# Gates taken straight from PSUM by tanh and product, and prompt scores held 2^7 larger, in a two-layer streaming encoder

## The chip, the cores and the metric

The kernel runs on one core of a Trainium2 chip. A core has TensorE (PE: matrix products from SBUF into PSUM), VectorE (DVE), ScalarE (ACT: one function per element, with a scale and a bias), GpSimd (POOL), and SyncE (SP), whose queue issues the DMA transfers here. Each engine works through its own queue in order and waits on semaphores for the others. The metric is the device time of one execution in microseconds.

## The reference

Two attention layers run one after the other on 2048 prompt tokens and 64 sample tokens with 1024 features. Each layer is

```
h = rms_norm(x, norm_g);  q, k, v, gate = split(h @ w_in)
q, k = rms_norm per head (64 wide)
s = q k^T / 8 + bias;  p = softmax(s)           (layer A: with a learned sink per head in the sum)
y = x + ((p v) * silu(gate)) @ w_out
```

Layer A has 16 query heads on 2 key heads; a 64-token chunk sees itself and 2 chunks before it. Layer B has 16 heads each with its own keys, and sees itself and 8 chunks before it. The outputs are y for both kinds of tokens and the newest rows of keys and values. silu(g) is g * (1 + tanh(g / 2)) / 2.

## The kernel before

Every product is made of high and low halves (fp32r pairs in layer A, fp16 pairs in layer B), so a projection of 128 tokens to 512 columns is 24 matmuls (`project`, lines 679 to 681). Layer A goes through four head groups `qd`, each over all units of 256 tokens; the first of them (`qd` 0) projects keys and values too, so that there a 256-column k/v projection and a 512-column q/gate projection alternate. Layer B goes through eight head pairs `hp`, each over all units; one projection gives q, k, v and gate of two heads, 128 columns each. Both write into the PSUM tile `pj`, of which there are two banks.

**The order of the work.** TensorE's order is written out by hand: attention steps of item x, and between them projection matmuls of later items (`filler.to`). All other engines' orders are set by a scheduler that simulates the program. Small side tasks (splitting weights, normalising heads, the gate) go through a list, `bg.put(cost, fn)`, with a cost each; `bg.share` runs some of it at each attention step, urgent ones first, and `queries` or `scores` force what an item still lacks.

**From the projection to the scores.** In layer A, `evacuate` (L702) copies q and gate from `pj` to `pa` and `pb`, scaled by the token's RMS factor `rr` on ScalarE. In layer B, `evacuate_b` copies q and k to `pa` (L715), the value's high half (L719), the value's low half on VectorE (L720), and then the gate to `pb` (L723). The scheduler's tool orders any two engines that touch one PSUM bank, so these four follow one another where the engine changes. `head_norm` squares on POOL (L756), sums on VectorE (L757), raises to -1/2 on POOL (L761) and multiplies on VectorE (L774). `gate` is a tanh of `pb` into a buffer `sq` on ScalarE (L782) and a product (tanh + 1) * gate on VectorE (L783).

`queries` transposes normalised q and k on TensorE (L844, tile `tp`) and writes them as fp16 halves with factors `qf`, `kf` per feature. `scores` in each layer makes the products (L1139 and L1140; L1416 and L1417, tile `sb`), adds the bias and takes the minimum of the negated scores in one VectorE instruction with a constant scale of 1.0 (L1150, L1420, results `p` and `nm`), and exponentiates on ScalarE (L1156, L1429). The row sums `sm` are inverted (L1161, L1437; in layer B, L1440 multiplies some by 2^14), and POOL multiplies them into the gate (`G`: L1163, L1448). The probabilities are transposed by TensorE (into `sa` or `sb`, split by L813, L814, L816, L817) or, for one head of each pair, split by L1463 and POOL's L1464 and transposed by DMA. `sb` has two buffers, for scores, transposed probabilities and transposed gates together.

`constants` (lines 136 to 154) makes the factors at the start; `scale_work` runs `input_across`, `input_scales` and `everywhere` once for each head pair, beside the work of the pair before. `bias_vectors_a` and `bias_vectors_b` make the negated bias vectors once.

Of the kernel before, what the change touches and what calls it, by code (L numbers as in the profile page):

```python
# [12 lines left out]
I32 = mybir.dt.int32  # L13
AF = mybir.ActivationFunctionType
# [42 lines left out]
def hybrid_encoder_kernel(  # L57
# [70 lines left out]
    qf = const([P, 2], "qf")  # L128
    kf = const([P, 2], "kf")
    kgr = const([P, 2, 2 * HD], "kgr")  # L130
    sink = const([P, 16], "sink")
    nsink = const([P, 16], "nsink")
    tab = const([P, 16], "tab")
    held = {}

    def constants():
# [8 lines left out]
        nc.vector.tensor_tensor(qf, qsc, ksc, op=ALU.mult)  # L145
        nc.vector.tensor_scalar(kf.bitcast(I32), qf.bitcast(I32), 0x7F800000, None, op0=ALU.bitwise_and)
        nc.vector.tensor_scalar(kf, kf, 0.125, 1.0, op0=ALU.mult, op1=ALU.max)
        nc.vector.tensor_scalar(kf, kf, 2.0 ** 15, 1.0, op0=ALU.min, op1=ALU.mult)
        inv = t("ms", [P, 8])[:, 0:2]
        nc.vector.reciprocal(inv, kf)  # L150
        nc.vector.tensor_tensor(qf, qf, inv, op=ALU.mult)
        nc.vector.tensor_scalar(qf, qf, 60000.0, -60000.0, op0=ALU.min, op1=ALU.max)
# [5 lines left out]
    scl = const([P, 9, 3], "scl")  # L158
    gsb = const([P, 8, KC], "gsb")
    S_W, C_B, G_B = (lambda h, i=i: scl[:, h, i : i + 1] for i in range(3))  # L160
    S_WO, S_OG, C_O = (scl[:, 8, i : i + 1] for i in range(3))
# [22 lines left out]

    def times(dst, a, c):
        nc.vector.tensor_scalar(dst, a, c, 1.0, op0=ALU.mult, op1=ALU.mult)

    def largest(j, a, b):
# [20 lines left out]

    def everywhere(h, o):  # L210
        ps = psum("tp", 512, 1)
        nc.tensor.matmul(ps[:, 0:3], ones[0:1, 0:1].to_broadcast([1, P]), o, start=True, stop=True)
        nc.vector.tensor_copy(scl[:, h], ps[:, 0:3])

# [5 lines left out]
    def input_across(h):  # L220
        across(h, h + 1)
        e, r, o = row[:, 16:17], row[:, 17:18], row[:, 20:23]
        powers(row[:, h : h + 1], e, r)
        times(o[:, 0:1], r, WB_)
        times(o[:, 1:2], e, 1 / (HB * WB_))
        times(o[:, 2:3], e, 0.5 / VB if h > 0 and len(TURNED) == 2 else 0.5 / (VB * PB))

    def input_scales(h):
        everywhere(h, row[:, 20:23])
        nc.vector.tensor_scalar(gsb[:, h], gain[:, 1, :], S_W(h), 1.0, op0=ALU.mult, op1=ALU.mult)  # L230
# [57 lines left out]
    def bias_vectors_a():  # L288
        oh = held["oh"]
        ps = psum("tp", 512, 1)  # L290
        nc.tensor.matmul(ps[:16, :VL], tab[:32, :16], oh[:32, :VL], start=True, stop=True)
        held["va"] = va = t("row", [P, VL], 2)
        nc.vector.tensor_scalar(va[:16, :VL], ps[:16, :VL], -1.0, 1.0, op0=ALU.mult, op1=ALU.mult)

    def bias_vectors_b():
        held["vb"] = vb = t("res", [P, 2 * OT], 2)
        vr = t("res", [P, 2 * OT], 2)
        load(vr[:16, :257], rel_rev)
        nc.vector.memset(vb[:16, 0:127], 0.0)
        nc.vector.tensor_scalar(  # L300
            vb[:16, 127:383], vr[:16, 0:256], vr[:16, 0:1], -1.0, op0=ALU.subtract, op1=ALU.mult
        )

    def keep(layer):
# [116 lines left out]

    bg = Background()

    def load_weights(g, *specs, scale=None):
# [183 lines left out]

    rr = [const([P, NT + 1], f"rms{l}") for l in range(2)]

    def token_scales(unit, x, ps):
# [7 lines left out]
    def sums_to_scales(layer, tt, parts, ps):  # L619
        w = len(parts)  # L620
        for i, part in enumerate(parts):
            nc.tensor.matmul(ps[:, 2 * i : 2 * i + 2], part, ones, start=True, stop=True)
        v = t("ms", [P, 8])
        nc.vector.tensor_scalar(
            v[:, : 2 * w], ps[:, : 2 * w], 1.0 / D, EPS, op0=ALU.mult, op1=ALU.add
        )
        nc.gpsimd.tensor_tensor(
            rr[layer][:, tt : tt + w],
            v[:, : 2 * w].rearrange("p (i e) -> p i e", e=2)[:, :, 0],
            mhalf[:, :w],  # L630
            op=ALU.pow,
        )

    def token_rows(unit):
# [11 lines left out]
    def row_scales(unit):  # L646
# [17 lines left out]
        nc.vector.tensor_scalar(v[:, :w], v[:, :w], 1.0 / D, EPS, op0=ALU.mult, op1=ALU.add)  # L664
        nc.gpsimd.tensor_tensor(rr[0][:, tt : tt + w], v[:, :w], mhalf[:, :w], op=ALU.pow)

    def project(tile_, xc, w, C, res, ps=None):
# [19 lines left out]

    def evacuate(layer, tt, n, ps, C, G, b=None):
        a = t("pa", [P, 384], 4)
        pieces = [(a[:, : C - G], ps[:, : C - G])]  # L690
        if G:
            out = a
            if b is None:
                b = t("pb", [P, 256], 5)
                out = a, b
            pieces.append((b[:, :G], ps[:, C - G : C]))
        else:
            out = a
        sc = rr[layer][:, tt : tt + 1]
        for dst, src in pieces:  # L700
            if n == P:
                held["evac"] = nc.scalar.activation(dst, src, AF.Identity, scale=sc).ins  # L702
            else:
                nc.scalar.activation(dst[:n], src[n:], AF.Identity, scale=sc[n:])
        if n < P:
            for dst, src in pieces:
                nc.vector.scalar_tensor_tensor(
                    dst[:n], src[:n], sc[:n], dst[:n], op0=ALU.mult, op1=ALU.add
                )
        return out  # L710

    def evacuate_b(hp, tt, ps, g):
        a = t("pa", [P, 384], 4)
        true = a if tt >= NT - 4 else a[:, 0:256]
        nc.scalar.activation(true, ps[:, : true.shape[1]], AF.Identity, scale=C_B(hp))  # L715
# [3 lines left out]
        nc.scalar.activation(vh[:, :, 0:HD], v, AF.Identity, scale=c)  # L719
        nc.vector.scalar_tensor_tensor(  # L720
            vh[:, :, HD:P], v, c, vh[:, :, 0:HD], op0=ALU.mult, op1=ALU.subtract
        )
        held["evac"] = nc.scalar.activation(g, ps[:, 384:512], AF.Identity, scale=C_B(hp)).ins  # L723
        return a
# [120 lines left out]

    halves = [slice(0, 64), slice(64, 128)]

    QS = const([P, 4, P], "QS", F32R)
# [62 lines left out]
    def layer_a():  # L911
# [4 lines left out]
        def add_unit(qd, place, unit):  # L916
# [193 lines left out]
        def scores(it):  # L1110
# [33 lines left out]
            for j in range(2):  # L1144
# [4 lines left out]
                for h in (2 * j, 2 * j + 1):  # L1149
                    mi = nc.vector.tensor_tensor_reduce(  # L1150
                        out=pv[:n, h % 2, :nk], in0=Sv[h][:n, :nk], in1=bias[h][:n, b0 : b0 + nk],
                        op0=ALU.add, op1=ALU.min, scale=1.0,
                        scalar=nsink[:n, 4 * qd + h : 4 * qd + h + 1], accum_out=nm[:n, h : h + 1],
# [6 lines left out]
            bg.anchor(mi, ex)  # L1160
            nc.vector.reciprocal(sm[:n], sm[:n])  # L1161
            it.G = G = t("G", [P, 256])
            nc.gpsimd.tensor_tensor(  # L1163
# [92 lines left out]
    def layer_b():  # L1256
# [4 lines left out]
        def add_unit(hp, unit):  # L1261
# [21 lines left out]
            def gen():  # L1283
# [9 lines left out]
                for e, (tt, t0, n) in enumerate(tiles):  # L1293
# [89 lines left out]
        def scores(it, i, h):  # L1383
# [35 lines left out]
            for r, b, c in soft:  # L1419
                mi = nc.vector.tensor_tensor_reduce(  # L1420
                    out=p[r, :nk], in0=S[r, o : o + nk], in1=b,
                    op0=ALU.add, op1=ALU.min, scale=1.0, scalar=3e38, accum_out=it.nm[r, c : c + 1],
                )
# [12 lines left out]
            if c == w - 1:  # L1436
                nc.vector.reciprocal(it.sm[:n, :w], it.sm[:n, :w])  # L1437
                if turned(it, 0) and len(TURNED) == 1:
                    part = it.sm[:n, TURNED[0] : w : 2]
                    nc.vector.tensor_scalar(part, part, PB, 1.0, op0=ALU.mult, op1=ALU.mult)  # L1440
                it.G = G = t("G", [P, 256])
# [480 lines left out]
```

## Time and profile before

| | us |
|---|---|
| median of 3 runs | 2210.4 (2204.73 to 2212.95) |
| the profiled execution | 2214.94 |
| its span | 2213.1 |
| TensorE busy | 2102.7 |
| VectorE busy | 1563.9 |
| ScalarE busy | 1425.7 |
| POOL busy | 1004.9 |

Layer A's attention runs from about 50 to 700 us, its output projection to about 850, layer B's attention from 870 to 2030, and the last output projection to the end. In rows of groups the columns are: line, engine, operation, output and inputs by name, shapes and count, then total busy us and mean ns of one, then the engine's idle time just before them and what ended it. In rows of waits: the engine and line that waited, for which engine and line, us in total, how often, and the longest.

### The profile page before, as it was taken

How to read it: one execution, taken by the hardware profiler on the slowest of the kernel's cores; microseconds unless marked ns; L12 is line 12 of the kernel's file. 1: busy time of each engine (PE TensorE's matmuls, PEld its weight loads, DVE VectorE, ACT ScalarE, POOL GpSimd, SP SyncE). 2: the span in 40 equal slices, each digit the busy share in tenths (PEclk: the TensorE clock that was granted, in tenths of full speed). 3: DMA queues.
4: the chain of work that ended last, by engine and by line, in shares of the span. 5: the costliest groups of instructions: out<-in, count | busy, mean ns of one | idle time of the engine just before them, and what ended most of it. 6: DMA issues, size and time to landing. Idle time of an engine off the chain costs nothing. (4 is left out here: it accounts for less than half of the span.)

```text
span 2213.1 us, 41369 instructions
## 1 busy us (share of the span) xinstructions
PE 2102.7 (95%) x13441; PEld 1522.1 (69%) x13441; DVE 1563.9 (71%) x4105; ACT 1425.7 (64%) x3610; POOL 1004.9 (45%) x1509
## 2 busy tenths in 40 slices
PE   7999999999999999989999999999999998998999
PEld 6887888788889997556555555555555555556888
DVE  6769777677676456778676777877767778677642
ACT  6878878777785333666666766766667667576420
POOL 5645544334454455853444444444454445443000
PEclk9999999999999999999999999999999999999999
DMA  8856546856546667545465565654756546345664
GB/s 274 275 162 215 179 127 219 234 160 195 170 129 184 210 204 244 171 143 167 107 186 133 130 177 130 173 148 121 186 133 155 159 111 172 91 104 136 199 200 124
DMA packets 383096, 372.87 MB, mean 168 GB/s; under 512 B 174672, under 2 KB 320352, under 8 KB 382848
## 3 DMA queue, kind: packets, MB, share of 16 engines
q1 hardware_dynamic: 382880, 370.23, 58.0%
q8 instruction: 106, 1.74, 0.3%
q14 instruction: 110, 0.90, 0.1%
HBM read 257.59 MB, written 73.43 MB: 150 GB/s over the span
## 5 line engine op out<-in xcount | busy, mean ns | idle before, releaser
L679 PE MATMUL pj<-wh,xx 128*128 128x512 f16 (+2 forms) x1648 | 643.4, 390 | 5.8 <-ACT pb L702 4.1
L681 PE MATMUL pj<-wh,xx 128*128 128x512 f16 (+2 forms) x1648 | 625.5, 380 | 2.5 <-POOL xx L564 2.5
L680 PE MATMUL pj<-wh,xx 128*128 128x512 f16 x1024 | 391.5, 382 | 0.0
L1429 ACT ACTIVATE p<-p,nm 128x640 f32<-128x640 f32 (+5 forms) x264 | 198.9, 753 | 213.6 <-DVE nm L1420 108.0
L1765 PE MATMUL pj<-xx,wh 128*128 128x264 f32 (+1 forms) x1024 | 290.0, 283 | 8.5 <-DVE res L1775 4.1
L1766 PE MATMUL pj<-xx,wh 128*128 128x264 f32 (+1 forms) x1024 | 287.7, 281 | 0.0
L1464 POOL TENSOR_TENSOR values<-p,values 128x640 f16<-128x640 f32 (+2 forms) x112 | 140.0, 1250 | 243.5 <-ACT values L1463 243.5
L680 PE MATMUL pj<-wl,xx 128*128 128x512 f32 (+1 forms) x624 | 233.9, 375 | 2.2 <-DVE wl L470 2.2
L564 POOL TENSOR_TENSOR xx<-xraw,xx 128x528 fp32r<-128x528 f32 (+4 forms) x144 | 184.9, 1303 | 87.8 <-ACT xx L563 74.6
L1420 DVE CUSTOM_DVE_ANT_0 p<-sb,BT 128x640 f32<-128x640 f32 (+5 forms) x272 | 195.6, 719 | 38.3 <-PE sb L1417 35.6
L1250 POOL TENSOR_TENSOR o<-gt,o 128x256 f32<-128x256 f32 (+1 forms) x132 | 101.1, 766 | 206.2 <-ACT p L1156 89.6
L761 POOL TENSOR_TENSOR f<-f,mhalf 128x4 f32<-128x4 f32 (+2 forms) x187 | 187.0, 1000 | 13.8
L681 PEld LDWEIGHTS <-xx 128*128 128x128 f16 x1024 | 100.9, 99 | 125.9 <-issue 3.9
L774 DVE TENSOR_TENSOR pa<-pa,f 128x256 f32<-128x256 f32 (+3 forms) x221 | 136.5, 618 | 55.1 <-POOL f L761 50.6
L1156 ACT ACTIVATE p<-p,nm 128x257 f32<-128x257 f32 (+2 forms) x272 | 134.3, 497 | 50.1 <-DVE nm L1150 41.7
L756 POOL TENSOR_TENSOR sq<-pa 128x256 f32<-128x256 f32 (+2 forms) x187 | 123.7, 663 | 72.5 <-ACT pa L715 38.2
L679 PEld LDWEIGHTS <-xx 128*128 128x128 f16 x1024 | 101.0, 99 | 71.5 <-issue 2.7
L680 PEld LDWEIGHTS <-xx 128*128 128x128 f16 x1024 | 100.9, 99 | 70.3 <-issue 2.9
L817 DVE SCALAR_TENSOR_TENSOR pl<-sb,ph 128x640 f16<-128x640 f32 (+4 forms) x144 | 106.2, 737 | 58.2 <-ACT ph L816 56.5
L1767 PE MATMUL pj<-xx,wl 128*128 128x264 f32 x512 | 145.0, 283 | 1.0 <-DVE wl L463 1.0
L1767 PE MATMUL pj<-xx,wh 128*128 128x264 f16 x512 | 142.1, 277 | 1.3 <-DVE wh L460 1.3
L1150 DVE CUSTOM_DVE_ANT_0 p<-sa,BT,nsink 128x256 f32<-128x256 f32 (+2 forms) x272 | 117.3, 467 | 34.6 <-PE sa L844 29.5
(273 smaller groups left out, 5290.7 us busy)
## 6 DMA issues: line engine op xcount, KB each, us to landing
xx<-xsb SPq DMA_DIRECT2D x112, 512.0 KB, 4.2
xx<-xsa SPq DMA_DIRECT2D x88, 512.0 KB, 4.8
xraw<-oga SPq DMA_DIRECT2D x64, 264.0 KB, 3.6
xraw<-ogb SPq DMA_DIRECT2D x64, 264.0 KB, 3.6
xsa<-xx SPq DMA_DIRECT2D x32, 512.0 KB, 4.0
scan<-in_w_in_b_dram SPq DMA_DIRECT2D x64, 256.0 KB, 4.6
wl<-in_w_in_b_dram SPq DMA_DIRECT2D x64, 256.0 KB, 4.0
xraw<-in_x_dram SPq DMA_DIRECT2D x40, 256.0 KB, 3.9
```

The lines of the kernel that those rows point to most:

```text
L564: nc.gpsimd.tensor_tensor(lo, rv, wide(hi), op=ALU.subtract)
L679: nc.tensor.matmul(ps[:n, :C], xh, wh, start=k == 0, stop=False)
L680: nc.tensor.matmul(ps[:n, :C], xh, wl, start=False, stop=False)
L681: nc.tensor.matmul(ps[:n, :C], xl, wh, start=False, stop=k == KC - 1)
L761: nc.gpsimd.tensor_tensor(fv, fv, mhalf[:n, :H], op=ALU.pow)
L774: nc.vector.tensor_tensor(sv, sv, fv.unsqueeze(2).to_broadcast([n, H, HD]), op=ALU.mult)
L1420: mi = nc.vector.tensor_tensor_reduce(out=p[r, :nk], in0=S[r, o : o + nk], in1=b, op0=ALU.add, op1=ALU.min, scale=1.0, scalar=3e38, accum_ ...
L1429: ex = nc.scalar.activation(p[:n, :nk], p[:n, :nk], AF.Exp, scale=-1.0, bias=it.nm[:n, c : c + 1], accum_out=it.sm[:n, c : c + 1],)
L1464: lo = nc.gpsimd.tensor_tensor(two[:, :, 1, :], pv, two[:, :, 0, :], op=ALU.subtract)
L1765: nc.tensor.matmul(ps[:, :OT], wh, oh, start=k == 0, stop=False)
L1766: nc.tensor.matmul(ps[:, :OT], wh, ol, start=False, stop=False)
L1767: nc.tensor.matmul(ps[:, :OT], wl, oh, start=False, stop=k == KC - 1)
```

## The change

1. **Gates.** For whole 128-token tiles the copy of the gate is gone. `gate_of` takes tanh on ScalarE straight from `pj` into a new buffer `e` (one of it), and VectorE multiplies (tanh plus or minus 1) with the gate, again straight from `pj`. The missing scale is put elsewhere: in layer A the tanh's scale is `nhalf`, which POOL makes from `rr` (`halve`), and the row sums get a factor -`rr`; in layer B the tanh's scale is a fourth column `H_B` of the scales, and the factor G_B, which already multiplies the transposed gate, takes the rest. In layer A the order stays q then gate; in layer B gate comes first, then q and k, then v. Side tasks `gate` remain only for tiles with fewer tokens. The 2^14 on the row sums (L1440) moves into G_B.
2. **Scores.** Factors `up`, `down` and `nup` are worked out at the start from the largest gains (a power of two, at most 2^7). q and the bias vectors are multiplied by `up`; the score reduction's scale becomes `down`, one value per partition, in place of 1.0. The factor's limits for `kf` change with it.

```
+        both = t("res", [P, 2 * OT], 2)[:, : 4 * P].rearrange("p (d c) -> p d c", c=4)
+        load(both, qk_gain.partition_broadcast(P))
+        nc.vector.tensor_tensor(both[:, :, 0:2], both[:, :, 0:2], both[:, :, 2:4], op=ALU.mult)
+        nc.vector.tensor_reduce(
+            up, both[:, :, 0:2].rearrange("p d c -> p c d"), axis=AX.X, op=ALU.max,
+            apply_absolute_value=True,
+        )
+        exponent(up, up)
+        nc.vector.tensor_scalar(up, up, 2.0 ** 10, 1e-20, op0=ALU.mult, op1=ALU.max)
+        nc.vector.reciprocal(up, up)
+        nc.vector.tensor_scalar(up, up, 2.0 ** 29 * 2.0 ** 7, 2.0 ** 7, op0=ALU.mult, op1=ALU.min)
+        nc.vector.reciprocal(down, up)
+        times(nup, up, -1.0)
+        nc.vector.tensor_tensor(qsc, qsc, up, op=ALU.mult)
...
     def everywhere(h, o):
...
+        if 0 < h < 8 and len(TURNED) == 1:
+            r = scl[halves[TURNED[0]], h, 2:3]
+            times(r, r, PB)
...
+    def halve(tt, w):
+        nc.gpsimd.tensor_tensor(nhalf[:, tt : tt + w], rr[0][:, tt : tt + w], mhalf[:, :w], op=ALU.mult)
...
+    def gate_of(ps, scale, g, one=1.0):
+        W = g.shape[1]
+        e = t("e", [P, 256], 1)[:, :W]
+        held["evac"] = nc.scalar.activation(e, ps, AF.Tanh, scale=scale).ins
+        nc.vector.scalar_tensor_tensor(g, e, one, ps, op0=ALU.add, op1=ALU.mult)
+
+    def evacuate(layer, tt, n, ps, C, G):
         a = t("pa", [P, 384], 4)
+        b = t("pb", [P, 256], 5) if G else None
+        sc = rr[layer][:, tt : tt + 1]
+        if n == P:
+            held["evac"] = nc.scalar.activation(a[:, : C - G], ps[:, : C - G], AF.Identity, scale=sc).ins
+            if G:
+                gate_of(ps[:, C - G : C], nhalf[:, tt : tt + 1], b[:, :G], -1.0)
+            return (a, b) if G else a
...
     def evacuate_b(hp, tt, ps, g):
         a = t("pa", [P, 384], 4)
         true = a if tt >= NT - 4 else a[:, 0:256]
+        gate_of(ps[:, 384:512], H_B(hp), g)
         nc.scalar.activation(true, ps[:, : true.shape[1]], AF.Identity, scale=C_B(hp))
...
-        held["evac"] = nc.scalar.activation(g, ps[:, 384:512], AF.Identity, scale=C_B(hp)).ins
...
-                it.todo += head_norm(n, it.pr[:n, 0:256], qd > 0) + gate(n, it.gate[:n])
+                it.todo += head_norm(n, it.pr[:n, 0:256], qd > 0)
+                if n < P:
+                    it.todo += gate(n, it.gate[:n])
...
-                        op0=ALU.add, op1=ALU.min, scale=1.0,
+                        op0=ALU.add, op1=ALU.min, scale=down[:n, 0:1],
...
+            if n == P:
+                nc.vector.tensor_scalar(
+                    sm, sm, rr[0][:, tt : tt + 1], -1.0, op0=ALU.mult, op1=ALU.mult
+                )
...
-                    it.todo += head_norm(n, pr[:n, 0:256]) + gate(n, it.gate[:n, e])
+                    it.todo += head_norm(n, pr[:n, 0:256])
...
-                    op0=ALU.add, op1=ALU.min, scale=1.0, scalar=3e38, accum_out=it.nm[r, c : c + 1],
+                    op0=ALU.add, op1=ALU.min, scale=down[r, 1:2], scalar=3e38, accum_out=it.nm[r, c : c + 1],
...
-                if turned(it, 0) and len(TURNED) == 1:
-                    part = it.sm[:n, TURNED[0] : w : 2]
-                    nc.vector.tensor_scalar(part, part, PB, 1.0, op0=ALU.mult, op1=ALU.mult)
```

More of the change, by code (lines that the diff above doesn't have):

```diff
@@ L134, in hybrid_encoder_kernel, with times, exponent @@
     held = {}
+    def times(dst, a, c):
+        nc.vector.tensor_scalar(dst, a, c, 1.0, op0=ALU.mult, op1=ALU.mult)
+    def exponent(dst, a):
+        nc.vector.tensor_scalar(
+            dst.bitcast(I32), a.bitcast(I32), 0x7F800000, None, op0=ALU.bitwise_and
+        )
     def constants():
@@ L157, in hybrid_encoder_kernel @@
     top = const([P, 12], "top")
-    scl = const([P, 9, 3], "scl")
+    scl = const([P, 9, 4], "scl")
     gsb = const([P, 8, KC], "gsb")
-    S_W, C_B, G_B = (lambda h, i=i: scl[:, h, i : i + 1] for i in range(3))
+    S_W, C_B, G_B, H_B = (lambda h, i=i: scl[:, h, i : i + 1] for i in range(4))
     S_WO, S_OG, C_O = (scl[:, 8, i : i + 1] for i in range(3))
@@ L210, in everywhere @@
     def everywhere(h, o):
+        w = o.shape[1]
         ps = psum("tp", 512, 1)
-        nc.tensor.matmul(ps[:, 0:3], ones[0:1, 0:1].to_broadcast([1, P]), o, start=True, stop=True)
-        nc.vector.tensor_copy(scl[:, h], ps[:, 0:3])
+        nc.tensor.matmul(ps[:, :w], ones[0:1, 0:1].to_broadcast([1, P]), o, start=True, stop=True)
+        nc.vector.tensor_copy(scl[:, h, :w], ps[:, :w])
+        if 0 < h < 8 and len(TURNED) == 1:
+            r = scl[halves[TURNED[0]], h, 2:3]
+            times(r, r, PB)
     def input_top(h):
@@ L221, in input_across @@
         across(h, h + 1)
-        e, r, o = row[:, 16:17], row[:, 17:18], row[:, 20:23]
+        e, r, o = row[:, 16:17], row[:, 17:18], row[:, 20:24]
         powers(row[:, h : h + 1], e, r)
@@ L225, in input_across @@
         times(o[:, 1:2], e, 1 / (HB * WB_))
-        times(o[:, 2:3], e, 0.5 / VB if h > 0 and len(TURNED) == 2 else 0.5 / (VB * PB))
+        times(o[:, 2:3], o[:, 1:2], 0.5 / VB if h > 0 and len(TURNED) == 2 else 0.5 / (VB * PB))
+        nc.vector.tensor_tensor(o[:, 2:3], o[:, 2:3], e, op=ALU.mult)
+        times(o[:, 3:4], o[:, 1:2], 0.5)
     def input_scales(h):
-        everywhere(h, row[:, 20:23])
+        everywhere(h, row[:, 20:24])
         nc.vector.tensor_scalar(gsb[:, h], gain[:, 1, :], S_W(h), 1.0, op0=ALU.mult, op1=ALU.mult)
@@ L422, in hybrid_encoder_kernel @@
     bg = Background()
+    halves = [slice(0, 64), slice(64, 128)]
     def load_weights(g, *specs, scale=None):
@@ L632, in sums_to_scales @@
         )
+        if layer == 0:
+            halve(tt, w)
     def token_rows(unit):
@@ L665, in row_scales @@
         nc.gpsimd.tensor_tensor(rr[0][:, tt : tt + w], v[:, :w], mhalf[:, :w], op=ALU.pow)
+        halve(tt, w)
     def project(tile_, xc, w, C, res, ps=None):
@@ L686, in project @@
         return cost
-    def evacuate(layer, tt, n, ps, C, G, b=None):
-        a = t("pa", [P, 384], 4)
+    def gate_of(ps, scale, g, one=1.0):
[4 more added lines that the diff above has]
+    def evacuate(layer, tt, n, ps, C, G):
+        a = t("pa", [P, 384], 4)
+        b = t("pb", [P, 256], 5) if G else None
[5 more added lines that the diff above has]
+            return (a, b) if G else a
         pieces = [(a[:, : C - G], ps[:, : C - G])]
         if G:
[L692 to L695, printed above, removed]
             pieces.append((b[:, :G], ps[:, C - G : C]))
-        else:
-            out = a
-        sc = rr[layer][:, tt : tt + 1]
         for dst, src in pieces:
[L701 to L710, printed above, removed]
+            nc.scalar.activation(dst[:n], src[n:], AF.Identity, scale=sc[n:])
+        for dst, src in pieces:
+            nc.vector.scalar_tensor_tensor(
+                dst[:n], src[:n], sc[:n], dst[:n], op0=ALU.mult, op1=ALU.add
+            )
+        return (a, b) if G else a
     def evacuate_b(hp, tt, ps, g):
```

24 lines of the change are left out of this document (14 added, 10 removed).

## The prediction

> **What bounds the kernel now.** I read the page's engine totals first, then busy time by stage, then whom TensorE waited for, then the groups by shape that the change touches, and last the timelines of the start and of one normalisation chain.
>
> The page, engine totals and granted clock:
>
> ```profile
> span 2213.1 us, 41369 instructions
> PE 2102.7 (95%) x13441; PEld 1522.1 (69%) x13441; DVE 1563.9 (71%) x4105; ACT 1425.7 (64%) x3610; POOL 1004.9 (45%) x1509
> PEclk9999999999999999999999999999999999999999
> ```
>
> TensorE is busy 2102.7 of 2213.1 us at full clock; the change adds or removes no matmul of a projection, score or output. So it can only move the 110.4 us in which TensorE stands. Where these lie (columns: stretch, its length, busy time of PE, PEld, DVE, ACT, POOL with instruction counts, clock, DMA share, GB/s):
>
> ```profile
> 0.00:50.00 50.00, 36.30 (x197) 29.97 (x198) 36.45 (x114) 33.82 (x77) 28.39 (x43) 0.97 0.88 279
> 50.00:200.00 150.00, 145.85 (x896) 123.47 (x895) 107.45 (x404) 121.22 (x339) 83.71 (x127) 0.99 0.68 215
> 200.00:700.00 500.00, 494.73 (x2848) 407.67 (x2847) 371.01 (x1070) 385.98 (x1065) 231.73 (x425) 1.00 0.59 179
> 870.00:2030.00 1160.00, 1090.34 (x6680) 654.19 (x6681) 872.26 (x2212) 772.18 (x1942) 569.04 (x837) 0.99 0.55 147
> ```
>
> Start-up: 13.7 us idle. Layer A from 200 on: 5.3, nothing to win. Layer B's attention: 69.7 us. Who let TensorE go, in layer B (870 to 2030) and then before 200 us:
>
> ```profile
> PE sb L844 <- DVE nm L1420: 14.0, 7, 2.3
> PE sb L1416 <- DVE nm L1420: 12.7, 10, 1.7
> PE sb L844 <- DVE pl L817: 10.2, 14, 1.4
> PE tp L844 <- DVE pa L774: 9.4, 7, 1.7
> ...
> PE sb L844 <- ACT values L719: 2.3, 1, 2.3
> ...
> PE tp L844 <- ACT gt L1237: 1.7, 2, 1.5
> PE sb L844 <- ACT gt L1237: 1.5, 3, 0.9
> ```
>
> ```profile
> PE pj L679 <- ACT pb L702: 4.1, 3, 2.1
> ...
> PE pj L680 <- DVE wl L470: 2.2, 1, 2.2
> ```
>
> In layer B it is VectorE that ends the waits: scores reduced (L1420), low halves (L817), normalised q/k (L774). ScalarE ends 5.5 us of them. So time taken off ScalarE pays only through VectorE's queue, and time put on VectorE can cost directly.
>
> **ScalarE, part by part.** Rows of the groups (busy us, mean ns | idle before):
>
> ```profile
> L723 ACT ACTIVATE pb<-pj,scl 128x128 f32<-128x128 f32 x128 | 46.6, 364 | 63.7 <-DVE values L720 60.9 <-DVE scrow L202 1.2
> L782 ACT ACTIVATE sq<-pb 128x128 f32<-128x128 f32 x128 | 38.4, 300 | 0.6
> L702 ACT ACTIVATE pb<-pj,rms 128x256 f32<-128x256 f32 x64 | 30.1, 470 | 0.0
> L782 ACT ACTIVATE sq<-pb 128x256 f32<-128x256 f32 x64 | 26.8, 419 | 2.8 <-DVE f L765 1.6
> ```
>
> Each 128-token tile had a gate evacuation and, later, a tanh of the copy. Now one tanh reads PSUM with a scale read per partition. I price it as the evacuation it replaces (same shape, same kind of scale): 364 ns in B, 470 in A. So the old tanhs' price leaves: 128 x 300 ns + 64 x 419 ns = 65.2 us less ScalarE, 38.4 of it in B.
>
> **VectorE.** Rows of its groups:
>
> ```profile
> L783 DVE SCALAR_TENSOR_TENSOR pb<-sq,pb 128x128 f32<-128x128 f32 x128 | 55.6, 434 | 20.5 <-ACT sq L782 20.3
> L720 DVE SCALAR_TENSOR_TENSOR values<-pj,values 128x128 f16<-128x128 f32 x128 | 36.5, 285 | 2.9 <-ACT values L719 1.4
> L783 DVE SCALAR_TENSOR_TENSOR pb<-sq,pb 128x256 f32<-128x256 f32 x64 | 32.6, 510 | 12.8 <-ACT sq L782 12.2
> L1771 DVE SCALAR_TENSOR_TENSOR res<-pj,scl,res 128x264 f32<-128x264 f32 x64 | 31.1, 490 | 71.7 <-PE pj L1767 50.4 <-DMA res<-x 20.8
> L1775 DVE TENSOR_TENSOR res<-pj,res 128x264 f32<-128x264 f32 x64 | 27.0, 427 | 52.9 <-PE pj L1767 52.8
> L1150 DVE CUSTOM_DVE_ANT_0 p<-sa,BT,nsink 128x256 f32<-128x256 f32 x240 | 106.4, 479 | 31.2 <-PE sa L844 27.3 <-PE sa L1140 1.9
> L1420 DVE CUSTOM_DVE_ANT_0 p<-sb,BT 128x256 f32<-128x256 f32 x16 | 6.7, 419 | 0.2
> L1440 DVE TENSOR_SCALAR sm<-sm 128x2 f32<-128x2 f32 x56 | 10.0, 178 | 1.3
> ```
>
> The product (tanh+1) times gate had two SBUF inputs; now one input is PSUM. The nearest rows with a PSUM input: 285 ns for 128 columns (L720) against 434, 427 for 264 columns (L1775) against 510. That is 128 x 149 + 64 x 83 ns = 24.4 us less. [...] The rows here are means amid other work and I take them.
>
> The scale of the score reduction turns from the constant 1.0 into a value per partition. L1150, which has one such operand, costs 60 ns more than L1420 at the same 256 columns; L1771 against L1775 says 63. At 63 ns for 272 calls that is 17.1 us in each layer (in A it is the second such operand: 0 to 63, I take 63). The new factor on sm in A: 64 x 178 ns = 11.4; the one removed in B: 10.0. Sums: A 17.1 + 11.4 - 5.3 = +23.2; B 17.1 - 10.0 - 19.1 = -12.0 us. A's 23 hide beside TensorE, which stood only 5.3 us after 200. In B only what stands on a wait counts: 17 waits name L1420, 17 x 0.063 = **+1.1** (0 to 17.1, every call on the path).
>
> **ScalarE's relief in B**, 38.4 us of 772. Direct waits on it are 5.5 us, and the L817 waits (10.2) follow a ScalarE cast; I take a fifth of these 15.7: **-3** (0 to -18, half of the 36.9 of the three uppermost waits).
>
> **Order and release in B.** The order was q/k evacuation, v, v's low half on VectorE, gate. Now it is tanh, product on VectorE, q/k, v, low half. L723's row shows that ScalarE does not read the bank while VectorE does: it stood 60.9 us behind L720, 0.48 per tile over 128. So q/k now come later by a tanh, a product and such a wait: 0.36 + 0.29 + 0.48 = 1.13 us. Queued behind the waiting evacuation are v's and the exponentials; behind the q/k are POOL's squares, the factor and L774, for which TensorE waited 7 times. One such chain, ScalarE, POOL, VectorE and TensorE rows:
>
> ```profile
> 1177.59 0.47 ACT L715 ACTIVATE pa<-pj,scl 128x256 f32<-128x256 f32 x1
> ...
> 1181.09 1.40 POOL L1464 TENSOR_TENSOR values<-p,values 128x640 f16<-128x640 f32 x1 [7.04 <-ACT values L1463]
> 1182.44 1.19 POOL L756 TENSOR_TENSOR sq<-pa 128x256 f32<-128x256 f32 x2
> ...
> 1186.91 0.69 DVE L175 TENSOR_REDUCE most<-scan 128x1 f32<-128x512 f32 x1 [1.92 <-DMA scan<-in_w_in_b_dram]
> 1187.52 0.60 DVE L774 TENSOR_TENSOR pa<-pa,f 128x256 f32<-128x256 f32 x1
> ...
> 1188.17 0.44 PE L844 MATMUL tp<-ident,pa 128*128 128x128 f32 x2 [1.58 <-DVE pa L774]
> ```
>
> Here the square stood over 4 us behind POOL's L1464 and L774 behind a scan's transfer: q/k 1.13 later would cost nothing. So half of 7 x 1.13: **+4** (0, to 15 items paying it whole, 17).
>
> [...]
>
> **Release in A.** The projection's bank was free after ScalarE's gate copy (L702 pb); now after VectorE's product. In the first quarter k/v and q/gate projections alternate on two banks, and TensorE already waited 3 times for pb. Each grows by product and queue, 0.43 + 0.48 = 0.9: **+3** (-1.4, a third of the 4.1, as ScalarE reaches it earlier; to 15, all 17 tiles). Layer A's q copy still comes first there, so its chain does not move.
>
> **Start-up.** Nine more VectorE instructions in `constants`, two of 256 elements, and one 256 KB load. Where VectorE is on the path:
>
> ```profile
> 12.44 0.15 DVE L145 TENSOR_TENSOR qf<-qsc,ksc 128x2 f32<-128x2 f32 x1
> ...
> 14.12 0.40 DVE L591 TENSOR_TENSOR o<-res 128x256 f32<-128x256 f32 x1
> ...
> 24.70 1.52 DVE L591 TENSOR_TENSOR o<-res 128x256 f32<-128x256 f32 x1
> ```
>
> 7 x 0.16 + 2 x 0.40 = 1.9, in a stage where TensorE stood 2.2 us for VectorE's wl (L470). **+2** (0 if they fall into a gap; 4.1 with the 1.52 rows, plus 0.9 for 256 KB at 279 GB/s: 5). The extra load is one more issue on SP's queue ahead of weights, inside that 0.9. POOL's `halve`, nine small products, lies before the tanh alone, after q's evacuation: 0. The few 1x1 operations per head pair and the extra products on the bias vectors: 0, a unit ahead of their use.
>
> **Sum:** 2 + 3 + 4 + 1.1 - 3 = +7.1 us. The profiled execution took 2214.94 us (span 2213.1 and 1.8 around it), 4.5 above the median 2210.4 of the runs shown; against it the sum gives 2222.0, against the median 2217.5: I say **2217**.
>
> **Rivals.** One, slower: the hand-over ScalarE, VectorE, ScalarE stands on TensorE's path in B. Price 1.13 us per item; I count 3.5 items, from 7 the sum passes 0.5%, and 15 give 17 for my 4, a sum of +20: about 2231. For it: 7 waits already there, 60.9 us of the same hand-over; against it: the chain above.
>
> Two, faster: ScalarE's relief reaches VectorE's queue, whose casts come sooner, and halves the 36.9 us of B's three largest waits: -18.5 in place of -3, and release and order cost nothing (+3 left): 2195. For it stands how long VectorE waited for ScalarE's casts in B:
>
> ```profile
> DVE pl L817 <- ACT ph L816: 55.0, 58, 1.8
> ```
>
> Against it: ScalarE was idle a third of B, so its work rarely came late through load.
>
> Three, no effect: both engines idle enough to take up every shift, only start-up's 2 remains: 2212.
>
> **Chances.** Forecast 0.36 (0.06 of it past the upper 0.5%), slower rival 0.34, faster rival 0.20 (0.02 within), no effect 0.10. About 0.5%, 11 us, is what a measurement of this kernel can tell from no change. Slower 0.06 + 0.34 = 0.40; faster 0.18; within 0.30 + 0.10 + 0.02 = 0.42. The forecast's own range is 2207 to 2226; the wide one, 2196 to 2239, leaves out a tenth at each end.
>
> **What would show it.** ScalarE's busy time falls by about 65 us; no evacuation into pb and no tanh from pb is left for whole tiles. The reductions into nm cost 60 ns more; if not, the 1.1 goes. The q/k evacuation (pa from pj) in B waits on the product instead of L723 on values; the product's mean lies near 285 in B. If TensorE's waits for normalised pa in B stay under 14 us, the hand-over is covered; above 25 it is rival one. Waits for nm and pl falling below 25 us speak for rival two. The forecast fails if the order that the scheduler gives VectorE's and ScalarE's queues shifts by more than these terms.

## The result and the profile after

The changed kernel takes 2234.1 us (median of 6 runs, 2224.1 to 2240.4) where the kernel before takes 2209.1 (median of 6, 2204.7 to 2213.3): a ratio of 1.0109, 95% interval [1.0082, 1.0136], about 24 us slower. The profiled execution took 2234.35 us. In the experiments below every ratio is to the kernel before, run beside it on the same chip, since the median of the kernel before itself lies between 2209 and 2221 from one set of runs to the next.

The page's engine totals of the changed kernel:

```profile
span 2232.6 us, 41200 instructions
PE 2113.7 (95%) x13441; PEld 1527.0 (68%) x13441; DVE 1576.1 (71%) x4146; ACT 1383.0 (62%) x3418; POOL 994.1 (45%) x1518
```

ScalarE has 192 instructions fewer, VectorE is 12 us busier (the prediction's A +23.2 and B -12.0 make 11.2), the matmuls are the same 13441. Yet TensorE is busy 11.0 us longer; the rest of the span's +19.5, 8.5 us, is idle time.

As TensorE's order is written out by hand, the n-th matmul is the same one in both traces, and the difference of their starts, each counted from the start of its span, tells when time is lost: +3.5 us at 50 us, +1.8 at 200, +4.5 at 870, +16.8 at 960, +22.2 at 2030, +19.4 at the last matmul. So 12.3 us go in 90 us, at the start of layer B's first head pair. Busy time in this stretch, in the columns of the prediction, first of the changed kernel, then of the kernel before:

```profile
870.00:960.00 90.00, 71.71 (x375) 39.37 (x374) 58.39 (x124) 42.37 (x106) 55.66 (x64) 0.89 0.54 182
```

```profile
870.00:960.00 90.00, 80.36 (x449) 45.62 (x450) 66.11 (x148) 52.56 (x136) 66.45 (x77) 0.94 0.55 182
```

Every engine does less in it, 74 matmuls fewer on TensorE, and the clock is lower, 0.89 against 0.94. Whom TensorE waited for, in the changed kernel, over the whole span (us in total, times, longest):

```profile
PE tp L884 <- DVE pa L814: 20.0, 7, 9.0
PE sb L1460 <- DVE nm L1464: 16.0, 13, 2.0
...
PE tp L884 <- DVE scl L236: 8.3, 5, 2.0
```

The same two waits for `pa` and `scl` in the kernel before:

```profile
PE tp L844 <- DVE pa L774: 11.0, 8, 1.7
...
PE tp L844 <- DVE scl L213: 1.3, 5, 0.3
```

The wait for normalised q/k (L774 before, L814 now) rose from 11.0 to 20.0 us, and one of its 7 waits is 9.0. The wait for `scl` (the copy of the next head pair's scales out of PSUM, where they have been spread over the partitions; L213 before, L236 now) was 1.3 us in 5 and is 8.3. Here is the 9.0. The rows of its chain on POOL, VectorE and TensorE, from the changed kernel's timeline:

```profile
903.12 0.41 DVE L797 TENSOR_REDUCE f<-sq 128x4 f32<-128x256 f32 x1
904.89 1.27 POOL L591 TENSOR_TENSOR xraw<-xraw,rows 128x512 f32<-128x512 f32 x1 [2.85 <-DMA xraw<-x]
906.11 1.16 POOL L595 TENSOR_TENSOR xx<-xraw,xx 128x512 f16<-128x512 f32 x1
907.22 0.21 POOL L800 TENSOR_TENSOR f<-f,small 128x4 f32<-128x4 f32 x1
907.37 3.38 POOL L595 TENSOR_TENSOR xx<-xraw,xx 128x512 f16<-128x512 f32 x3
910.70 1.02 POOL L801 TENSOR_TENSOR f<-f,mhalf 128x4 f32<-128x4 f32 x1
911.75 0.83 DVE L814 TENSOR_TENSOR pa<-pa,f 128x256 f32<-128x256 f32 x1 [3.60 <-POOL f L801]
912.73 0.66 PE L884 MATMUL tp<-ident,pa 128*128 128x128 f32 x2 [8.99 <-DVE pa L814]
```

And POOL and TensorE at the same tile in the kernel before:

```profile
895.08 0.24 POOL L760 TENSOR_TENSOR f<-f,small 128x4 f32<-128x4 f32 x1
895.40 1.01 POOL L761 TENSOR_TENSOR f<-f,mhalf 128x4 f32<-128x4 f32 x1
897.12 1.27 POOL L560 TENSOR_TENSOR xraw<-xraw,rows 128x512 f32<-128x512 f32 x1 [0.72 <-DMA xraw<-x]
```

```profile
898.80 0.44 PE L844 MATMUL tp<-ident,pa 128*128 128x128 f32 x2 [0.87 <-DVE pa L774]
```

Before, the two tiny POOL steps of the head norm (an addition and the power -1/2, on 4 columns) came first, and the scaling and splitting of the next tokens (L560, L564) followed. Now the scheduler has put them the other way round: the sum is ready at 903.5, but the addition waits till 907.2 behind a product that itself stands 2.85 us for its transfer, and the power behind three splits, till 910.7. Some 7 us of a chain that holds 1.2 us of POOL's work, and TensorE stands at its end.

The second place occurs in later head pairs, where the next pair's scales are spread; four times the copy stands as shown here. VectorE and TensorE, changed kernel:

```profile
1407.85 1.61 DVE L814 TENSOR_TENSOR pa<-pa,f 128x256 f32<-128x256 f32 x1 [1.40 <-POOL f L801]
1409.38 0.15 DVE L236 COPY scl<-tp 128x4 f32<-128x4 f32 x1
```

```profile
1409.59 0.66 PE L884 MATMUL tp<-ident,pa 128*128 128x128 f32 x4 [2.01 <-DVE scl L236]
```

The copy of 0.15 us frees the one PSUM tile `tp` for the next transposes. It stands behind a normalisation that waits for POOL and then runs 1.61 us; TensorE waits for the copy. In the kernel before, the instruction ahead of the copy at these places is a sum of 0.42 us (L757).

### The profile page after: what moved, and what is told of

Its sections match the earlier page's. It is cut to its first block, busy times and chain, and to the rows that moved or that the text cites. A ratio compares the mean times of both kernels' runs of the same rounds, so it can differ in the third digit from the quotient of the medians.

```text
span 2232.6 us, 41200 instructions
## 1 busy us (share of the span) xinstructions
PE 2113.7 (95%) x13441; PEld 1527.0 (68%) x13441; DVE 1576.1 (71%) x4146; ACT 1383.0 (62%) x3418; POOL 994.1 (45%) x1518
## 4 chain that ended last, share of the span: by engine, by line
PE 44%; DVE 12%; DMA 7%; ACT 6%; issue 4%; POOL 4%; SPq 1%; POOLq 0%; ACTq 0%; DVEq 0%
PE pj L717 6%; PE pj L719 6%; PE pj L718 6%; DMA scan<-in_w_in_b_dram 4%; PE pj L1806 4%; PE pj L1808 4%; PE pj L1807 4%; DVE p L1464 2%; PE sb L884 2%; PE o L1641 2%; PE sb L1460 1%; DVE pa L814 1%; PE sb L1461 1%; PE o L1602 1%; ACT p L1473 1%
## 5 line engine op out<-in xcount | busy, mean ns | idle before, releaser
L1464 DVE CUSTOM_DVE_ANT_0 p<-sb,BT,down 128x640 f32<-128x640 f32 (+5 forms) x272 | 211.9, 779 | 28.0 <-PE sb L1461 25.1
L796 POOL TENSOR_TENSOR sq<-pa 128x256 f32<-128x256 f32 (+2 forms) x187 | 117.5, 630 | 169.7 <-ACT pa L756 101.9
L814 DVE TENSOR_TENSOR pa<-pa,f 128x256 f32<-128x256 f32 (+3 forms) x221 | 124.7, 564 | 49.8 <-POOL f L801 45.5
L1190 DVE CUSTOM_DVE_ANT_0 p<-sa,BT,nsink 128x256 f32<-128x256 f32 (+2 forms) x272 | 134.3, 528 | 21.3 <-PE sa L884 17.6
```

The costliest lines, as they stand in the source:

```text
L814: nc.vector.tensor_tensor(sv, sv, fv.unsqueeze(2).to_broadcast([n, H, HD]), op=ALU.mult)
L1464: mi = nc.vector.tensor_tensor_reduce(out=p[r, :nk], in0=S[r, o : o + nk], in1=b, op0=ALU.add, op1=ALU.min, scale=down[r, 1:2], scalar=3e3 ...
```

## The experiments

The first theory is that gate-first in layer B costs by moving tiny instructions in the in-order queues, not by its own durations. The rivals are the scores' new work, layer A's later release of the projection bank, and the hand-over itself (the prediction's 1.13 us per item). The expectations of the first four runs use the word "hand-over" for the later q/k together with the long wait that grows from it, and set a "reshuffle" against it: any shift of the queues makes a stall somewhere.

**Gate last in B.** All of the change, with layer B's gate in its old place:

```
     def evacuate_b(hp, tt, ps, g):
...
-        gate_of(ps[:, 384:512], H_B(hp), g)
         nc.scalar.activation(true, ps[:, : true.shape[1]], AF.Identity, scale=C_B(hp))
...
+        gate_of(ps[:, 384:512], H_B(hp), g)
         return a
```

> The changed kernel with one line moved: in layer B tanh and product come last, after q/k, v and v's low half, where the gate copy stood before. Theory hand-over (q/k come later by a tanh, a product and a wait, and one such delay near 900 us grows to the 9.0 us wait and a half clock): some 12 us less than the change, about 2222 us, no TensorE wait over 4 us for normalised pa. Theory score scale (the per-partition scale and the longer start cost the time): as the changed kernel, 2234. Theory reshuffle (any shift of the queues makes such a stall somewhere): anything, with a long wait at another place.

Measured: 2211.0 us, ratio 0.9969 [0.9958, 0.9980]. The same instructions in another order are 1.4% faster than the changed kernel (0.9969 against 1.0109) and beat the kernel before. That is 28 to 31 us for the place of the gate, where some 12 were expected, so more than the one long wait goes with it. Both waits are back to about their size before, 11.0 and 1.3, and no wait for `pa` is over 1.9 us (rows of TensorE's waits):

```profile
PE tp L884 <- DVE pa L814: 10.2, 7, 1.9
PE sb L884 <- DVE pl L857: 9.9, 16, 1.7
PE sb L884 <- ACT gt L1281: 8.1, 5, 1.8
PE sb L1460 <- DVE nm L1464: 8.1, 12, 1.2
...
PE sb L884 <- DVE nm L1464: 4.8, 4, 2.4
...
PE tp L884 <- DVE scl L236: 1.3, 5, 0.3
```

**Gates alone.** Gates as changed (first in B), scores and constants as before:

```
...
-        both = t("res", [P, 2 * OT], 2)[:, : 4 * P].rearrange("p (d c) -> p d c", c=4)
...
-                        op0=ALU.add, op1=ALU.min, scale=down[:n, 0:1],
+                        op0=ALU.add, op1=ALU.min, scale=1.0,
...
-                    op0=ALU.add, op1=ALU.min, scale=down[r, 1:2], scalar=3e38, accum_out=it.nm[r, c : c + 1],
+                    op0=ALU.add, op1=ALU.min, scale=1.0, scalar=3e38, accum_out=it.nm[r, c : c + 1],
```

> Only the gates are changed; scores, constants and bias vectors as before. Hand-over: 2228 to 2232 us, the stall near 900 us is there, start-up as before. Score scale: 2209 to 2213. Reshuffle: between, with no relation to the place near 900 us.

Measured: ratio 1.0063 [1.0046, 1.0080], less than the 2228 to 2232 us expected (1.0086 to 1.0104 of 2209). The long wait is there without any of the scores' work:

```profile
PE tp L866 <- DVE pa L796: 21.3, 8, 9.1
```

**Scores alone.** The kernel before with `up`, `down` and `nup`; gates copied as before:

```
...
-            vb[:16, 127:383], vr[:16, 0:256], vr[:16, 0:1], -1.0, op0=ALU.subtract, op1=ALU.mult
+            vb[:16, 127:383], vr[:16, 0:256], vr[:16, 0:1], 1.0, op0=ALU.subtract, op1=ALU.mult
         )
+        times(vb[:16, 127:383], vb[:16, 127:383], nup[:16, 1:2])
...
-                        op0=ALU.add, op1=ALU.min, scale=1.0,
+                        op0=ALU.add, op1=ALU.min, scale=down[:n, 0:1],
...
```

> Only the scores are changed (up, down, nup and the constants); gates copied as before. Hand-over: 2212 to 2215 us, 2 to 4 us lost before 50 us and little after. Score scale: 2228 to 2234. Reshuffle: anything from 2205 to 2235.

Measured: ratio 1.0011 [0.9999, 1.0023], 2.4 us, which may be nothing; TensorE's waits for `scl` are 1.3 us. The scores' work is not the loss.

**B's gates copied.** The changed kernel, but layer B's gate is copied last and its tanh is a side task again (its factor G_B goes back with it):

```
...
-        gate_of(ps[:, 384:512], H_B(hp), g)
...
+        held["evac"] = nc.scalar.activation(g, ps[:, 384:512], AF.Identity, scale=C_B(hp)).ins
...
-                    it.todo += head_norm(n, pr[:n, 0:256])
+                    it.todo += head_norm(n, pr[:n, 0:256]) + gate(n, it.gate[:n, e])
```

> The changed kernel with layer B's gates copied and put through tanh as before; layer A's gates and all scores as changed. Hand-over: 2212 to 2217 us, with no stall near 900 us. Score scale: 2230 to 2234. Reshuffle: anything.

Measured: ratio 0.9990 [0.9979, 1.0002], a little less than the 2212 to 2217 us expected. So layer A's gates and the scores together cost nothing that can be measured; layer A's later release isn't the loss either. What is lost comes from layer B's gate, and "gate last" shows that it comes from its place.

The next four take the two places apart. They ran on one chip.

**The changed kernel once more**, with no edit, as the measure for the three below.

> The changed kernel as it is, on the chip of the next three. Both theories: 1.009 to 1.013 of the kernel before, the 9 us wait for normalised pa at its place near 900 us.

Measured: ratio 1.0094 [1.0068, 1.0121]; the waits for `pa` 20.2 us (longest 8.8) and for `scl` 8.3 are there again.

**POOL's power ahead of the splits.** Gate first everywhere; POOL's part of the token products and splits is ordered behind the last head-norm power issued:

```
...
-                        (nc.vector, nc.gpsimd)[c % 2].tensor_tensor(
+                        m = (nc.vector, nc.gpsimd)[c % 2].tensor_tensor(
...
+                        if c % 2:
+                            behind(m.ins, held["pow"])
...
+                    if rows is not None:
+                        behind(low.ins, held["pow"])
...
```

> The changed kernel, gate still first in layer B; POOL's splits of the first head pair's activations are only ordered behind the power of the head norm issued last before them. Theory POOL order (the later q/k let the power of one tile fall behind four splits that wait for a load and for ScalarE): the 9.0 us wait falls under 2 us and the time by 8 to 14 us against the changed kernel. Theory hand-over (the time goes with every tile's later q/k, wherever POOL's order lies): at most 3 us less.

Measured: ratio 1.0044 [1.0022, 1.0066], 11 us less than the unedited kernel beside it, and no wait for `pa` over 1.6 us, both as the theory of POOL's order had it. The timeline of POOL at that tile, and TensorE's waits:

```profile
901.33 1.51 POOL L805 TENSOR_TENSOR f<-f,mhalf 128x4 f32<-128x4 f32 x1
...
905.89 4.50 POOL L597 TENSOR_TENSOR xx<-xraw,xx 128x512 f16<-128x512 f32 x4
```

```profile
PE tp L888 <- DVE pa L818: 9.8, 7, 1.6
PE tp L888 <- DVE scl L236: 8.3, 5, 2.0
```

The gate is as early as in the changed kernel, and every hand-over ScalarE, VectorE, ScalarE is still paid; the edit mends POOL's order alone, and the 9 us wait is gone. The `scl` waits stay, as they have another cause.

**Gate last for the first head pair only, and gate first for it only.**

```
...
-        gate_of(ps[:, 384:512], H_B(hp), g)
+        if hp > 0:
+            gate_of(ps[:, 384:512], H_B(hp), g)
         nc.scalar.activation(true, ps[:, : true.shape[1]], AF.Identity, scale=C_B(hp))
...
+        if hp == 0:
+            gate_of(ps[:, 384:512], H_B(hp), g)
         return a
```

> The changed kernel with the gate last for the first head pair alone, first for the seven others. POOL order at the start of layer B: 12 to 17 us less than the changed kernel, up to 960 us as with the gate last everywhere, and the 5 us that are lost between 1000 and 1940 us remain. Hand-over in every tile: an eighth of what gate last gives everywhere, some 3 us.

Measured: ratio 1.0021 [1.0005, 1.0037], 16 to 18 us less than the changed kernel, the size of POOL's order and not the 3 us of a hand-over in every tile.

The two conditions exchanged:

```
...
-        gate_of(ps[:, 384:512], H_B(hp), g)
+        if hp == 0:
+            gate_of(ps[:, 384:512], H_B(hp), g)
         nc.scalar.activation(true, ps[:, : true.shape[1]], AF.Identity, scale=C_B(hp))
...
+        if hp > 0:
+            gate_of(ps[:, 384:512], H_B(hp), g)
         return a
```

> The gate first for the first head pair alone, last for the seven others. POOL order: 12 to 17 us more than with the gate last everywhere, all before 960 us. Hand-over in every tile: 3 us more than with the gate last everywhere.

Measured: ratio 1.0035 [1.0013, 1.0057], 15 us more than with the gate last everywhere, in the range of POOL's order. The waits part cleanly. With the gate last in the first pair only:

```profile
PE sb L1463 <- DVE nm L1467: 17.3, 14, 2.0
PE tp L887 <- DVE pa L817: 10.3, 7, 1.6
...
PE tp L887 <- DVE scl L236: 8.3, 5, 2.0
```

With the gate first in the first pair only:

```profile
PE tp L887 <- DVE pa L817: 20.2, 7, 8.3
...
PE sb L1463 <- DVE nm L1467: 7.9, 12, 1.2
...
PE tp L887 <- DVE scl L236: 1.3, 5, 0.3
```

Against 0.9969 with the gate last in all pairs, gate first costs 1.0035 - 0.9969 = 0.0066 in the first pair, 15 us, and 1.0021 - 0.9969 = 0.0052, 11 us, in the seven others together. The sum, 26 us, is what separates the changed kernel from gate-last (0.0125 to 0.0140, 28 to 31 us) within the intervals. In the others it shows as waits for `scl` (+7) and for the reduced scores `nm` (17.3 against 7.9). Why the waits for `nm` grow there was not settled: no run changed them alone, so the hand-over itself isn't ruled out as their cause.

The last four ask whether queue places explain the others too.

**q and k, then the gate, then the value.**

```
     def evacuate_b(hp, tt, ps, g):
...
+        nc.scalar.activation(true, ps[:, : true.shape[1]], AF.Identity, scale=C_B(hp))
         gate_of(ps[:, 384:512], H_B(hp), g)
-        nc.scalar.activation(true, ps[:, : true.shape[1]], AF.Identity, scale=C_B(hp))
```

> The changed kernel with layer B's order q/k copy, tanh, product, then v and its low half: only the q/k copy goes ahead of the gate. In the order that it fixes, POOL's power of the tile near 900 us stands ahead of the splits, as with the gate last, but VectorE's copy of the scales (scl from tp) still stands behind a normalisation of pa, as with the gate first. Theory queue places: the 9 us wait is gone and the 8 us of waits for scl stay; 6 to 9 us above the gate last, some 0.9995 to 1.002 of the kernel before. Theory hand-over (time goes with how late q/k are copied): equal to the gate last within 2 us.

Measured: ratio 1.0008 [0.9994, 1.0022]. Here q and k wait for no product at all. POOL's order is good and the long wait for `pa` is gone, yet it's 0.4% behind gate-last, as the theory of queue places had it:

```profile
PE sb L884 <- DVE nm L1464: 11.2, 9, 2.4
...
PE tp L884 <- DVE scl L236: 8.2, 5, 2.3
...
PE tp L884 <- DVE pa L814: 1.6, 2, 1.3
```

**Gate last, once more**, beside it on the same chip.

> The gate last in layer B once more, beside the other two on one chip: 0.996 to 0.998 of the kernel before.

Measured: ratio 0.9966 [0.9952, 0.9980], as the first time.

**Gates alone, gate last.** The kernel of "gates alone" with one more edit:

```
-        gate_of(ps[:, 384:512], H_B(hp), g)
         nc.scalar.activation(true, ps[:, : true.shape[1]], AF.Identity, scale=C_B(hp))
...
+        gate_of(ps[:, 384:512], H_B(hp), g)
         return a
```

> Gates straight from PSUM, in layer B last, with scores, constants and bias vectors as in the kernel before. If the score scale costs what it cost alone (0.001, within its interval of nothing to 0.0023): 1 to 5 us below the gate last with the score scale, 0.994 to 0.997 of the kernel before. If the scale per partition cost more once the gates no longer hide it: 6 to 12 us below.

Measured: ratio 0.9992 [0.9977, 1.0006], a miss: I expected it to be as fast as gate-last or faster, since it has less work. Two of its waits:

```profile
PE tp L866 <- DVE pa L796: 9.9, 8, 1.7
PE tp L866 <- DVE scl L219: 8.6, 5, 1.9
```

The scheduler has put the copy of the scales behind the normalisation here too, in five head pairs. The kernel with less VectorE work comes out 0.3% slower than the one with more (the two intervals just overlap): 0.0026, 5.8 us, with 7.3 us more of waits for `scl`. Other waits moved as well (those for `nm` fell from 12.9 to 4.2 us), so that the `scl` waits are the whole of it is argued and not shown. I had taken the gate's place for what decides the copy's place; it is one of several things that tip it. To this extent the "reshuffle" holds: a small edit elsewhere moved the copy too.

**The copy of the scales on ScalarE.** To test the copy by itself, the order of "q and k, then the gate" is kept and one instruction changes its engine:

```
     def everywhere(h, o):
...
-        nc.vector.tensor_copy(scl[:, h, :w], ps[:, :w])
+        nc.scalar.copy(scl[:, h, :w], ps[:, :w])
```

> Edit: the order q and k, tanh, product, value, low half of the run before it, and in addition the copy of the four scales out of the transposition tile (line 236) is done by ScalarE, in whose queue it stands right behind the tanh, and no longer by VectorE behind a normalisation. Theory of queue places: what keeps that order at 1.0008 while the gate at the end gives 0.997 is this small copy, so TensorE's five waits for scl fall from 8.2 us to under 4, and the ratio to the kernel before falls to 0.996 to 0.9985. Rival: the waits for scl are only where an unavoidable delay shows; they go, other waits grow as much, and the ratio stays at 0.9995 to 1.002.

Measured: ratio 0.9983 [0.9969, 0.9996], where the same order with the copy on VectorE gave 1.0008 [0.9994, 1.0022].

```profile
PE tp L884 <- ACT scl L236: 2.8, 5, 0.6
```

The waits fall from 8.2 to 2.8 us and the time by about 5.5 us (0.0025; the two intervals touch, so the size is rough). As the scheduler then orders VectorE's queue anew, the waits for `nm` (11.2 to 6.0 here) moved too, and part of the gain may be theirs.

Gate-last, at 0.9969 and 0.9966, remains the best version found, about 7 us better than the kernel before; the last run, at 0.9983, can't be told from it.

## Why the prediction was right or wrong, step by step

The time of 2234 lies in the wide range (2196 to 2239) but past the forecast's own (2207 to 2226): 24 us came where the sum had 7. The wide range holds it because rival one had a chance of 0.34. The size is that of rival one (2231), and the place too: q and k in layer B behind the product. Its mechanism is only half right, so that its price came so near is in part luck.

**Order and release in B, +4: the step that failed.** Against the gate last it measured 26 to 31 us. The working held that the square stood 4 us behind POOL's other work anyhow, "q/k 1.13 later would cost nothing", and priced what was left at 1.13 us per item. Both took the queues' order as given. What the runs show is that the 1.13 us tip the order: in the first head pair POOL's addition and power fall behind token splits (about 15 us, of which 11 come back when POOL's order alone is mended), and in the later ones VectorE's copy of the scales falls behind a normalisation, and waits for `nm` grow (about 11 us). The last sentence of the prediction had named it ("the order that the scheduler gives VectorE's and ScalarE's queues shifts by more than these terms"), though without a price, and without POOL's queue. The hand-over itself is there, as foreseen, and at `pa`, where the prediction looked for it, it costs nothing that shows. ScalarE's evacuation of q and k in layer B now stands behind the product,

```profile
ACT pa L756 <- DVE pb L730: 84.6, 78, 3.1
```

and with POOL's order mended TensorE's waits for `pa` are 9.8 us, no more than the 11.0 before. Whether it costs something at `nm` is open. The test set in advance (under 14 covered, above 25 rival one) gave 20.0, in between: one wait of 9.0 and six of 1.8 on average, so not "the price per item" at all.

**The premise, 110.4 us of idle time.** The prediction took TensorE to be at full clock (the mean was 0.991 in that execution) and the change to move only the time in which it stands. That did not hold: of the span's +19.5 us, 11.0 are busy time for the same matmuls, by estimate 6.1 of them because TensorE was busy at half clock for 46.4 us where it was 34.3 before. The last section gives the figures; no term of the sum had it.

**Start-up, +2:** the aligned matmuls are 3.5 us later at 50 us, inside the 0 to 5 that were given. Profiles differ here by several us: in all those with the new constants it is 2.3 to 6.9 us, in the two without them (gates alone) 1.9 and 0.8. So the size is right, and no single profile can tell it closer.

**Release in A, +3:** TensorE's waits for `pb` are 3.1 us in 4 against 4.1 in 3 before, and the delay shrinks from 3.5 to 1.8 us between 50 and 200 us (from 6.9 to 6.6 in the second profile of the same kernel). The term was 0 or a little below; its low end (-1.4) was nearer than its value. Of the 2.7 us lost from 200 to 870 I only know a row that grew there, waits for the transfer of q (2.1 to 6.1 us between 50 and 700).

**ScalarE.** The groups fell by what was worked out, tanh from PSUM at 366 ns in layer B against 364 taken (469 against 470 in A):

```profile
L729 ACT ACTIVATE e<-pj,scl 128x128 f32<-128x128 f32 x128 | 46.8, 366 | 44.0 <-PE pj L719 42.8
```

But the engine's busy time fell by 42.7 us, not 65. Durations of neighbours overlap in the records: all of ScalarE's add up to 1631.0 us before and 1566.9 now, 64.1 less, while the time covered by them fell from 1425.7 to 1383.0. So 65.2 us of groups weren't 65.2 us of queue.

The relief's -3 couldn't be seen alone. In the changed kernel the three waits for `nm` and `pl` are 16.0 + 1.7 + 9.7 = 27.4 us, above the 25 below which they were to speak for rival two. In gate-last they are 8.1 + 4.8 + 9.9 = 22.8 us against 36.9 before, and that version is 7 us faster than before; but its waits for the transposed gate `gt` are 8.8 us where they were 3.6. So a relief as in rival two may exist, of some 7 us in place of its 18.5, and at `nm` rather than at `pl`, which stayed at 10. That ScalarE's shorter queue is its cause is not shown: "gates alone, gate last" has the same ScalarE work and is only 0.9992, though with the long waits for `scl`, and no run shortened ScalarE's queue alone.

**VectorE's products and pointers.** Rows of groups of the changed kernel:

```profile
L730 DVE SCALAR_TENSOR_TENSOR pb<-e,pj 128x128 f32<-128x128 f32 x128 | 36.1, 282 | 20.7 <-ACT e L729 19.5
L1190 DVE CUSTOM_DVE_ANT_0 p<-sa,BT,nsink 128x256 f32<-128x256 f32 x240 | 121.5, 540 | 19.5 <-PE sa L884 16.1 <-PE sa L1180 1.9
L1464 DVE CUSTOM_DVE_ANT_0 p<-sb,BT,down 128x256 f32<-128x256 f32 x16 | 7.7, 480 | 0.3
```

The product costs 282 ns in layer B, 285 taken, against 434 with both inputs in SBUF (in A 417, 427 taken, against 510): the nearest row with a PSUM input was the right one to go by. The pointer scale costs +61 ns as the first such operand (419 to 480) and +61 as the second (479 to 540), 63 taken. The factor on the row sums (L1203) was mis-sized, 378 ns against 178; with layer B's gates copied, where it is still there, nothing of it shows in the time.

## What to carry to other kernels

Where an edit delays one chain by a microsecond and a scheduler orders the queues, don't price the microsecond: list the tiny instructions on that chain and the bulk work they could fall behind in each in-order queue, and take that work's length, and the transfer it may wait for, as the bound. When engines take turns at one PSUM bank, as ScalarE and VectorE do in the changed kernel (84.6 us of waits in 78), first read what TensorE waits for soonest, and last what nobody waits for, such as a gate; one line moved was 1.2 to 1.4% here. And after such an edit compare the order of the queues before durations: with the gate last, the version with less work came out the slower one.

## What was not expected of the hardware

The one long wait of TensorE cost, by estimate, about a quarter more than its length. Stretches of 2 us around the 9.0 us wait, in the columns of the stretches above (the clock is third from the end):

```profile
907.00:909.00 2.00, 0.00 (x0) 0.00 (x0) 0.44 (x2) 0.64 (x2) 2.00 (x4) 0.50 0.25 41
...
915.00:917.00 2.00, 2.00 (x7) 1.04 (x6) 1.82 (x4) 0.97 (x4) 0.69 (x1) 0.53 0.88 324
917.00:919.00 2.00, 2.00 (x12) 0.98 (x10) 1.91 (x5) 0.01 (x1) 0.00 (x0) 1.00 0.00 0
```

TensorE stands from 903.7. The granted clock falls to 0.50 at 906.64, about 3 us later, and stays there till 916.88, 4.15 us after the matmuls begin again at 912.73. In those 4 us matmuls of 512 columns start every 0.42 us, afterwards every 0.22, so half of the 4 us, an estimated 2, comes on top of the 9.0:

```profile
915.10 0.63 PE L718 MATMUL pj<-wh,xx 128*128 128x512 f16 x1
915.52 0.63 PE L719 MATMUL pj<-wh,xx 128*128 128x512 f16 x1
...
917.28 0.38 PE L717 MATMUL pj<-wh,xx 128*128 128x512 f16 x1
917.50 0.38 PE L718 MATMUL pj<-wh,xx 128*128 128x512 f16 x1
```

Shorter waits were followed by half clock too. In the kernel before, TensorE waits 2.19 us for `nm` until 1152.95 us, the clock is 0.50 from 1153.22 to 1156.63, and matmuls of 512 columns start every 0.43 us in that time; and after idle times of 1.23 and 1.00 us, the second over at 2013.26, it is 0.50 from 2013.38 to 2016.79. In the profiles of the kernel before and of the changed kernel the half clock comes in pieces of 3.41, 6.83 or 10.24 us, except for the last, which runs past the last instruction, and in each profile all of them begin on one grid of 3.41 us. Of this grid's pieces at full clock, the 16 in which TensorE was busy for under 0.40 of the time were all followed by half clock, those over 0.54 never, and 7 of the 23 between. So short waits that fall close together, or one of 2 us, can cost more than their length too.

TensorE worked at half clock for 34.3 us before and for 46.4 now, so that, by the spacing of the matmuls (0.42 us against 0.22), an estimated 17.2 and 23.2 us were lost: 6.1 of the 11.0 us by which its busy time grew for the same matmuls, some 2 of them behind the long wait. The rest of the 11.0 wasn't followed up, and between the profiles of this study these figures differ by several us (a mean clock of 0.984 in the second profile of the changed kernel, where the first has 0.987; busy time 2105.0 with the scores alone, 2112.2 with the gate last in the first pair). Over all runs the mean clock is 0.986 for the changed kernel, 0.988 with POOL's order mended and 0.989 to 0.990 for the kernel before.
